# A transformer block on one core: norms written over the projection's output, four row tiles in flight on VectorE, and the last two quarters of the output projection fused

## The chip, the cores and the metric

The kernel runs on one core of one Trainium2 chip. The metric is the device time of one execution in microseconds (us), as the median of several runs. The core's engines are TensorE (PE, matmuls), VectorE (DVE), ScalarE (ACT) and GpSimd (POOL); SyncE (SP) issues the DMAs. SBUF is the memory on the chip, PSUM the small memory that matmuls write.

## What is computed

One layer of a hybrid encoder block in float32: 1024 rows (SEQ) of 1024 channels (D_MODEL), feed-forward width 2816. Three sub-layers follow one another, each between an RMS norm before and an RMS norm behind it, and each is added to the residual stream:

```python
def rms_norm(x, g):
    xf = x.astype(jnp.float32)
    y = xf * lax.rsqrt(jnp.mean(xf * xf, axis=-1, keepdims=True) + EPS)
    return (y * g.astype(jnp.float32)).astype(x.dtype)
...
        f1 = swiglu(rms_norm(h, ffn1_pre_g[l]), ffn1_w_gate[l], ffn1_w_up[l], ffn1_w_down[l])
        h = h + 0.5 * rms_norm(f1, ffn1_post_g[l])
        mix = hybrid_mixer(rms_norm(h, mix_pre_g[l]), positions, w_in[l], b_gate[l],
...
        h = h + rms_norm(mix, mix_post_g[l])
        f2 = swiglu(rms_norm(h, ffn2_pre_g[l]), ffn2_w_gate[l], ffn2_w_up[l], ffn2_w_down[l])
        h = h + 0.5 * rms_norm(f2, ffn2_post_g[l])
```

The mixer projects its input once (`w_in`), runs a latent attention and a dilated windowed attention, merges the two by sigmoid gates and ends with the output projection `merged @ w_out`.

## The kernel before

**Tiling.** The 1024 rows are eight tiles (t = 0 to 7) of 128 rows; a half (hf) is four tiles, 512 rows. All products run in a 32-bit matmul format on numbers split in two, a high and a low part, with three matmuls per product (hi·hi, hi·lo, lo·hi). ScalarE copies the high part, VectorE or GpSimd subtracts it to get the low part. For activations this is `transpose_split` (L418 to L434): TensorE transposes four 128x128 blocks into a PSUM bank, ScalarE writes xh, VectorE writes xl (L433). For weights it is `split`: ScalarE, then GpSimd (L524).

**FFN.** Gate and up products are formed by a scheme of seven products in place of eight over blocks of x (class XS): blocks 0 to 2 are plain pieces of x, blocks 3 to 6 need differences between a tile of the second half and the tile four below it in the first half. For FFN2 the first half's normalised tile is stored in DRAM (xn_d) and read back (xo) for these differences (L416), which go to two slots xt per tile. The down projection accumulates over blocks into the eight output tiles acc (the tile y of the norms). Its last block reads the loads hp; each of its 16 groups of six matmuls is added to acc by VectorE (L1171), and then the tile's norm starts.

**Between two sub-layers** each tile goes through `postnorm` (L474): load the residual (res, SP's queue), ScalarE squares y and sums (L501), GpSimd takes the reciprocal root (L309, L311), the gain is multiplied in (L490) partly by GpSimd and partly by VectorE into a new slot xn, and VectorE forms res = xn · rstd + res (L514, the residual step), which is stored. Then `prenorm` (L436) does the same for the next sub-layer: square (L443), root, and scaling of res with rstd and the next gain. The columns up to `split_at` are scaled by VectorE in pieces (L453), the rest by ScalarE and GpSimd (L459, L460). Last come the transposes and splits of the tile. FFN1's norms (post1) lead to the mixer, the output projection's (`tail`) to FFN2, FFN2's (post2) to the output.

**Output projection** (`outproj`, L2572): for each half four quarters dd of the 1024 input channels. Each quarter gives, per tile and half of the columns, six matmuls into one bank; ScalarE copies the first quarter's result to y, VectorE adds the others (L2560). After the last quarter of a tile, its tail starts. Early products of FFN2 that need only the first tiles (the heads) fill in beside it.

**What sets the order.** The program is written by a planner (class Plan): processes ask for an engine with an estimated duration and a rank, wait for events, and take tokens. A simulated run of them writes the instructions of each engine in one fixed order, and each engine keeps to its order on the chip. `norm_tok` (L1248) holds how many tiles may be in the norms at once: two. `B1` holds four PSUM banks. Pool "u" has 21 slots of 4 KB per partition, for y, x, res, xn, xo, xt, gains and raw weights; an allocation waits until the slot's last user is done, and a load that waits for a slot holds what stands behind it on SP's queue. Constants PRE1 to PRE2 and POOL1 to POOL2 say how many columns of a tile go to which engine:

```python
PRE1, PREM, PRE2 = 768, 768, D
POOL1, POOLM, POOL2 = [512] * 8, [384] * 8, [512] * 4 + [1024, 768, 512, 512]
```

Of the kernel before, what the change touches and what calls it, by code (L numbers as in the profile page):

```python
# [107 lines left out]
PRE1, PREM, PRE2 = 768, 768, D  # L108
POOL1, POOLM, POOL2 = [512] * 8, [384] * 8, [512] * 4 + [1024, 768, 512, 512]
# [4 lines left out]
EARLY = 4  # L114
W0 = 4
# [106 lines left out]
def _build(tc, es, a, consts, out, dbg):  # L222
# [133 lines left out]
    class XS:  # L356
# [25 lines left out]
        def put(self, t, xn, scaled, rank):  # L382
# [7 lines left out]
            if hf == 0:  # L390
                self.nat[j] = (xs, scaled)
                for kb in range(2):
                    spawn(after(scaled[kb], self.block(kb, j, xs[kb])), rank)
                for ev in scaled:
                    yield ev
                if self.late is not None:
                    yield dma(512, lambda: load(xn_d[j * P : (j + 1) * P, :], xn))
            else:
                spawn(after(scaled[1], self.block(2, j, xs[1])), rank)
                old, olds = self.nat[j]  # L400
                if self.late is not None:
                    ob = []

                    def back():
                        o = slot([P, D], name="xo")
                        load(o, xn_d[j * P : (j + 1) * P, :])
                        ob.append(o)

                    yield dma(512, back)
                    old = [ob[0][:, 0:512], ob[0][:, 512:1024]]  # L410
                for ev in (*scaled, *olds):
                    yield ev
                tt = [slot([P, 2, 512], name="xt") for _ in range(2)]
                t1, t2, t3, t4 = tt[0][:, 0, :], tt[0][:, 1, :], tt[1][:, 0, :], tt[1][:, 1, :]
                for i, o, a_, b_ in ((4, t1, xs[0], old[0]), (5, t2, xs[1], t1), (6, t3, xs[1], xs[0]), (3, t4, old[1], t2)):
                    yield dve(512, lambda: V.tensor_sub(o, a_, b_))  # L416
                    spawn(self.block(i, j, o), rank)
# [18 lines left out]
    def prenorm(src, g, X, t, rank, split_at, xn=None):  # L436
# [12 lines left out]
        m = split_at  # L449
        scaled = [Event(), Event((m > 512) + (m < D))]  # L450

        def on_dve(c0, c1, ev):
# [5 lines left out]
        def on_pool(c0, c1, ev):  # L458
            yield act(c1 - c0, lambda: A.mul(xn[:, c0:c1], src[:, c0:c1], rs[0]))  # L459
            yield pool(c1 - c0, lambda: G.tensor_mul(xn[:, c0:c1], xn[:, c0:c1], g()[:, c0:c1]))  # L460
            plan.set(ev)

        spawn(on_dve(0, 512, scaled[0]), rank)
        if m > 512:
            spawn(on_dve(512, m, scaled[1]), rank)
        if m < D:
            spawn(on_pool(m, D, scaled[1]), rank)
# [5 lines left out]
    def postnorm(y, g, res_src, dst, t, box, junk, pool_cols, parts=1):  # L473
# [10 lines left out]

        m = pool_cols(t)
        gained = Event((m > 0) + (m < D))

        def gain_of(cols, eng):
            def write():
                eng.tensor_mul(xn[:, cols], y[:, cols], g()[:, cols])  # L490

            n = cols.stop - cols.start
            yield (pool if eng is G else dve)(n, write)
            plan.set(gained)

        xn = slot([P, D], name="xn")
        box.append(xn)
# [6 lines left out]
        if m:  # L504
            spawn(gain_of(slice(0, m), G), 0)
        if m < D:
            spawn(gain_of(slice(m, D), V), 8)
        yield act(D + 100, sq)
        yield from rstd_steps(bx[0], D, rs)
        yield gained  # L510
        n = D // parts
        for q in range(parts):
            cs = slice(n * q, n * q + n)
            yield dve(n, lambda: V.scalar_tensor_tensor(res[:, cs], xn[:, cs], rs[0], res[:, cs], op0=ALU.mult, op1=ALU.add))  # L514
# [709 lines left out]
    def begin():  # L1224
        def one(t):
# [9 lines left out]
            yield from prenorm(bx[0], lambda: gb["g1"], X1, t, 3, PRE1)  # L1235
# [12 lines left out]
    norm_tok = Tokens(2)  # L1248

    def post1(y, t):  # L1250
# [8 lines left out]
        yield from postnorm(y, lambda: gb["p1"], a["x"], h1, t, bx, lambda: gb["j1"], POOL1.__getitem__)  # L1259
        yield from prenorm(bx[0], lambda: gb["gm"], Xm, t, 3, PREM, bx[1])  # L1260
# [1193 lines left out]
    def merge():  # L2454
# [109 lines left out]
        def tail(y, t, ev):  # L2564
            yield ev
            yield norm_tok
            bx = []
            yield from postnorm(y, lambda: gb["pm"], h1, h2, t, bx, lambda: gb["jm"], POOLM.__getitem__)
            yield from prenorm(bx[0], lambda: gb["g2"], X2, t, 3, PRE2, bx[1])
            plan.release(norm_tok)  # L2570

        def outproj():  # L2572
# [5 lines left out]
            for hf, dd in blocks:  # L2578
                for c in (2 * dd, 2 * dd + 1):
                    yield mts[hf, c][1]  # L2580
                    yield wod[hf, c][1]
                if hf == 1 and dd == 1:
                    plan.set(out_started)
                for j in range(4):
# [3 lines left out]
                    if dd == 0:  # L2588
                        acc[t] = slot([P, D], name="y")
                    for n in range(2):  # L2590
# [4 lines left out]
                        def write():  # L2595
                            bs.ps = bank()
                            terms = []
                            for c in (2 * dd, 2 * dd + 1):
# [4 lines left out]
                        yield pe(6 * 512, write)  # L2603
                        spawn(evac(acc[t], dd == 0, ns, bs.ps, ev), 4)
                    if dd == 3:
                        spawn(tail(acc[t], t, ev), 5)
                plan.release(m_tok, 2)
                plan.release(wd_tok, 2)
# [11 lines left out]
    def post2(y, t):  # L2620
# [5 lines left out]
        yield from postnorm(y, lambda: gb["p2"], h2, out, t, [], lambda: gb["j2"], POOL2.__getitem__, 2 if t == NT - 1 else 1)  # L2626
# [40 lines left out]
```

## Time and profile before

| | us |
|---|---|
| median of 3 runs | 2434.36 |
| lowest and highest run | 2431.82, 2435.98 |
| the profiled execution's own time | 2432.88 |
| its span, first to last instruction | 2430.7 |
| TensorE busy | 2294.6 |
| VectorE busy | 1609.8 |
| ScalarE busy | 1044.0 |
| GpSimd busy | 784.1 |

The profile is of one execution. Its time, 2432.88 us, is its span and 2.2 us around it, and lies 1.5 us under the median. The mean granted clock of TensorE is 0.974 of full speed, 2.4 GHz; the lower level, 0.5, is 1.2 GHz. A row of a timeline gives the start, the duration, the engine, the line of the code, the operation, what it writes and reads, and in brackets how long the engine stood idle before it and what ended that. Several instructions of a kind in a row stand in one row.

### The profile page before, as it was taken

How to read it: one execution, taken by the hardware profiler on the slowest of the kernel's cores; microseconds unless marked ns; L12 is line 12 of the kernel's file. 1: busy time of each engine (PE TensorE's matmuls, PEld its weight loads, DVE VectorE, ACT ScalarE, POOL GpSimd, SP SyncE). 2: the span in 40 equal slices, each digit the busy share in tenths (PEclk: the TensorE clock that was granted, in tenths of full speed). 3: DMA queues.
4: the chain of work that ended last, by engine and by line, in shares of the span. 5: the costliest groups of instructions: out<-in, count | busy, mean ns of one | idle time of the engine just before them, and what ended most of it. 6: DMA issues, size and time to landing. Idle time of an engine off the chain costs nothing. (4 is left out here: it accounts for less than half of the span.)

```text
span 2430.7 us, 30689 instructions
## 1 busy us (share of the span) xinstructions
PE 2294.6 (94%) x11096; PEld 1920.7 (79%) x11096; DVE 1609.8 (66%) x2669; ACT 1044.0 (43%) x1952; POOL 784.1 (32%) x592
## 2 busy tenths in 40 slices
PE   6999999999979999999998898988979999999997
PEld 4788888788869987888886777776868888887885
DVE  7877878875672105666666766347787778778658
ACT  6233434431153336666655545454433334344111
POOL 2000000354274555756532322575300000006443
PEclk9999999999989999999999999999979999999998
DMA  6234434587352133122223222675533444357762
GB/s 186 83 130 139 173 127 163 195 321 254 134 173 70 62 98 100 38 72 65 61 82 90 79 73 85 194 258 180 182 108 113 163 140 173 116 197 280 259 238 104
DMA packets 197145, 350.17 MB, mean 144 GB/s; under 512 B 32577, under 2 KB 112961, under 8 KB 196481
## 3 DMA queue, kind: packets, MB, share of 16 engines
q1 hardware_dynamic: 196992, 348.21, 42.6%
q8 instruction: 87, 1.43, 0.2%
q14 instruction: 66, 0.53, 0.1%
HBM read 234.78 MB, written 113.38 MB: 143 GB/s over the span
## 5 line engine op out<-in xcount | busy, mean ns | idle before, releaser
L706 PE MATMUL s<-xh,wt 128*128 128x512 f32 x1408 | 453.8, 393 | 10.2 <-DVE uu L807 9.0
L524 POOL TENSOR_TENSOR wdb<-rawd,wdb 128x1024 fp32r<-128x1024 f32 x34 | 87.3, 2567 | 892.4 <-ACT wdb L523 889.3
L706 PE MATMUL b<-xh,wt 128*128 128x512 f32 x1056 | 345.7, 394 | 0.7 <-ACT xh L432 0.6
L706 PEld LDWEIGHTS s<-xh,wt 128*128 128x128 f32 x1408 | 266.2, 189 | 69.8 <-DVE uu L807 10.7
L706 PE MATMUL s<-xl,wt 128*128 128x512 f32 x704 | 275.7, 392 | 0.0
L706 PEld LDWEIGHTS b<-xh,wt 128*128 128x128 f32 x1056 | 200.9, 190 | 44.0 <-ACT xh L432 1.0
L706 PE MATMUL b<-xl,wt 128*128 128x512 f32 x528 | 207.7, 393 | 0.9 <-DVE xl L433 0.9
L1134 PE MATMUL b<-wdb,ha 128*128 128x512 f32 x864 | 202.5, 389 | 0.0
L1134 PE MATMUL s<-wdb,ha 128*128 128x512 f32 x816 | 190.5, 389 | 0.0
L1134 PEld LDWEIGHTS b<-wdb,ha 128*128 128x128 f32 x864 | 162.4, 188 | 33.8
L1134 PEld LDWEIGHTS s<-wdb,ha 128*128 128x128 f32 x816 | 153.1, 188 | 31.8
L1495 PE MATMUL b<-xh,wh 128*128 128x512 f32 x384 | 162.7, 424 | 1.4 <-DVE o L2016 0.8
L1966 POOL TENSOR_TENSOR p<-p,rd 128x1024 f32<-128x1024 f32 x64 | 122.5, 1923 | 117.7 <-DVE rd L1963 112.5
L706 PEld LDWEIGHTS s<-xl,wt 128*128 128x128 f32 x704 | 133.3, 189 | 27.4
L1495 PE MATMUL b<-xl,wh 128*128 128x512 f32 x384 | 153.2, 399 | 0.0
L675 ACT CAST wt<-s 128x512 fp32r<-128x512 f32 x176 | 104.2, 617 | 113.9 <-DVE s L635 59.0
L1495 PE MATMUL b<-xh,wl 128*128 128x512 f32 x384 | 152.9, 398 | 0.0
L524 POOL TENSOR_TENSOR wdb<-td,wdb 128x1024 fp32r<-128x1024 f32 x40 | 108.1, 2706 | 109.7 <-ACT wdb L523 98.6
L428 PE MATMUL b<-cst,p 128*128 128x128 f32 x768 | 107.2, 280 | 22.2 <-DVE ptd L433 14.9
L524 POOL TENSOR_TENSOR wl<-raw,wh 128x512 fp32r<-128x512 f32 (+3 forms) x88 | 110.0, 1267 | 53.5 <-ACT wh L523 46.5
L428 PEld LDWEIGHTS b<-cst,p 128*128 128x128 f32 x768 | 90.1, 143 | 40.0 <-DVE ptd L433 17.5
L676 DVE TENSOR_TENSOR wt<-s,wt 128x512 fp32r<-128x512 f32 x176 | 117.9, 684 | 5.4 <-ACT wt L675 5.1
(298 smaller groups left out, 4989.8 us busy)
## 6 DMA issues: line engine op xcount, KB each, us to landing
hs_d<-hl SPq DMA_DIRECT2D x112, 512.0 KB
ha<-hs_d SPq DMA_DIRECT2D x56, 1024.0 KB
raw<-in_ffn_w_gate_dram SPq DMA_DIRECT2D x48, 512.0 KB
raw<-in_ffn_w_up_dram SPq DMA_DIRECT2D x48, 512.0 KB
rawd<-in_ffn_w_down_dram SPq DMA_DIRECT2D x44, 512.0 KB
raw<-in_w_in_dram SPq DMA_DIRECT2D x28, 512.0 KB
h<-res SPq DMA_DIRECT2D x16, 512.0 KB
lg_d<-lg SPq DMA_DIRECT2D x32, 256.0 KB
```

The source lines that it names most:

```text
L428: T.transpose(b[:rows, i * P : (i + 1) * P], src(i), ident)
L524: yield pool(n, lambda: G.tensor_sub(lo, src, hi))
L675: yield act(512, lambda: A.copy(w[:, 0], src))
L676: yield dve(512, lambda: V.tensor_sub(w[:, 1], src, w[:, 0]))
L706: T.matmul(out(), l, r, start=(first and k == 0 and n == 0), stop=(k == 3 and n == 2), skip_group_check=True,)
L1134: T.matmul(ps, l, r, start=(fresh and n == 0), stop=(n == 5), skip_group_check=True)
L1495: T.matmul(bs.ps, l, r, start=(part == 0 and n == 0), stop=(part == 7 and n == 2))
L1966: yield pool(S, lambda: G.tensor_tensor(bx.p, bx.p, bx.rd.broadcast_to([P, S]), op=ALU.mult))
```

## The change

- `prenorm`: VectorE scales all columns in two pieces of 512. ScalarE's and GpSimd's part (L459, L460) and the constants are gone.
- `postnorm`: the gain is multiplied by one VectorE operation over 1024 columns into y itself; the slot xn is gone. The operation is asked for after ScalarE's square, which reads y. The next norm's squares and scaled values are written to y too.
- `norm_tok`: four tiles in the norms at once, not two.
- `XS.put`: two of the four differences are written over the tile read back from DRAM (old), so one slot xt per tile serves, not two.
- `outproj`: in the second half the last two quarters are taken together, 12 matmuls per bank and one addition by VectorE, tile by tile.

Line numbers after it are 21 lower than before from `postnorm`'s end on (1 lower around L428).

```diff
@@ -107,4 +107,2 @@
 
-PRE1, PREM, PRE2 = 768, 768, D
-POOL1, POOLM, POOL2 = [512] * 8, [384] * 8, [512] * 4 + [1024, 768, 512, 512]
 GATES_FROM = 4
@@ -114,2 +112,3 @@
 EARLY = 4
+NORM = 4
 W0 = 4
@@ -412,4 +411,4 @@
                     yield ev
-                tt = [slot([P, 2, 512], name="xt") for _ in range(2)]
-                t1, t2, t3, t4 = tt[0][:, 0, :], tt[0][:, 1, :], tt[1][:, 0, :], tt[1][:, 1, :]
+                tt = slot([P, 2, 512], name="xt")
+                t1, t2, t3, t4 = old[0], tt[:, 0, :], tt[:, 1, :], old[1]
                 for i, o, a_, b_ in ((4, t1, xs[0], old[0]), (5, t2, xs[1], t1), (6, t3, xs[1], xs[0]), (3, t4, old[1], t2)):
@@ -435,3 +434,3 @@
 
-    def prenorm(src, g, X, t, rank, split_at, xn=None):
+    def prenorm(src, g, X, t, rank, xn=None):
 
@@ -448,6 +447,5 @@
         xn = bx[0]
-        m = split_at
-        scaled = [Event(), Event((m > 512) + (m < D))]
+        scaled = [Event(), Event()]
 
-        def on_dve(c0, c1, ev):
+        def scale(c0, c1, ev):
             yield dve(c1 - c0, lambda: V.scalar_tensor_tensor(
@@ -457,12 +455,4 @@
 
-        def on_pool(c0, c1, ev):
-            yield act(c1 - c0, lambda: A.mul(xn[:, c0:c1], src[:, c0:c1], rs[0]))
-            yield pool(c1 - c0, lambda: G.tensor_mul(xn[:, c0:c1], xn[:, c0:c1], g()[:, c0:c1]))
-            plan.set(ev)
-
-        spawn(on_dve(0, 512, scaled[0]), rank)
-        if m > 512:
-            spawn(on_dve(512, m, scaled[1]), rank)
-        if m < D:
-            spawn(on_pool(m, D, scaled[1]), rank)
+        for n in range(2):
+            spawn(scale(512 * n, 512 * n + 512, scaled[n]), rank)
         yield from X.put(t, xn, scaled, rank)
@@ -472,3 +462,3 @@
 
-    def postnorm(y, g, res_src, dst, t, box, junk, pool_cols, parts=1):
+    def postnorm(y, g, res_src, dst, t, box, junk, parts=1):
 
@@ -483,16 +473,4 @@
         res = box[0]
-
-        m = pool_cols(t)
-        gained = Event((m > 0) + (m < D))
-
-        def gain_of(cols, eng):
-            def write():
-                eng.tensor_mul(xn[:, cols], y[:, cols], g()[:, cols])
-
-            n = cols.stop - cols.start
-            yield (pool if eng is G else dve)(n, write)
-            plan.set(gained)
-
-        xn = slot([P, D], name="xn")
-        box.append(xn)
+        box.append(y)
+        gained = Event()
 
@@ -503,7 +481,8 @@
 
-        if m:
-            spawn(gain_of(slice(0, m), G), 0)
-        if m < D:
-            spawn(gain_of(slice(m, D), V), 8)
+        def gain_of():
+            yield dve(D, lambda: V.tensor_mul(y, y, g()))
+            plan.set(gained)
+
         yield act(D + 100, sq)
+        spawn(gain_of(), 2)
         yield from rstd_steps(bx[0], D, rs)
@@ -513,3 +492,3 @@
             cs = slice(n * q, n * q + n)
-            yield dve(n, lambda: V.scalar_tensor_tensor(res[:, cs], xn[:, cs], rs[0], res[:, cs], op0=ALU.mult, op1=ALU.add))
+            yield dve(n, lambda: V.scalar_tensor_tensor(res[:, cs], y[:, cs], rs[0], res[:, cs], op0=ALU.mult, op1=ALU.add))
             spawn(store(dst[t * P : (t + 1) * P, cs], res[:, cs], 512 // parts), 6)
@@ -1234,3 +1213,3 @@
             yield gains0
-            yield from prenorm(bx[0], lambda: gb["g1"], X1, t, 3, PRE1)
+            yield from prenorm(bx[0], lambda: gb["g1"], X1, t, 3)
 
@@ -1247,3 +1226,3 @@
     tail1 = Event()
-    norm_tok = Tokens(2)
+    norm_tok = Tokens(NORM)
 
@@ -1258,4 +1237,4 @@
         bx = []
-        yield from postnorm(y, lambda: gb["p1"], a["x"], h1, t, bx, lambda: gb["j1"], POOL1.__getitem__)
-        yield from prenorm(bx[0], lambda: gb["gm"], Xm, t, 3, PREM, bx[1])
+        yield from postnorm(y, lambda: gb["p1"], a["x"], h1, t, bx, lambda: gb["j1"])
+        yield from prenorm(bx[0], lambda: gb["gm"], Xm, t, 3, bx[1])
         plan.release(norm_tok)
@@ -2567,4 +2546,4 @@
             bx = []
-            yield from postnorm(y, lambda: gb["pm"], h1, h2, t, bx, lambda: gb["jm"], POOLM.__getitem__)
-            yield from prenorm(bx[0], lambda: gb["g2"], X2, t, 3, PRE2, bx[1])
+            yield from postnorm(y, lambda: gb["pm"], h1, h2, t, bx, lambda: gb["jm"])
+            yield from prenorm(bx[0], lambda: gb["g2"], X2, t, 3, bx[1])
             plan.release(norm_tok)
@@ -2577,7 +2556,9 @@
             gb["jm"] = half_slot([P, D], mybir.dt.bfloat16, name="junk")
-            for hf, dd in blocks:
-                for c in (2 * dd, 2 * dd + 1):
+            turns_ = [(0, (d,)) for d in range(4)] + [(1, (0,)), (1, (1,)), (1, (2, 3))]
+            for hf, dds in turns_:
+                cc = [2 * d + u for d in dds for u in range(2)]
+                for c in cc:
                     yield mts[hf, c][1]
                     yield wod[hf, c][1]
-                if hf == 1 and dd == 1:
+                if hf == 1 and dds[0] == 1:
                     plan.set(out_started)
@@ -2587,3 +2568,3 @@
                     ev = Event(2)
-                    if dd == 0:
+                    if dds[0] == 0:
                         acc[t] = slot([P, D], name="y")
@@ -2597,3 +2578,3 @@
                             terms = []
-                            for c in (2 * dd, 2 * dd + 1):
+                            for c in cc:
                                 m, w = mts[hf, c][0].t, wod[hf, c][0]
@@ -2602,8 +2583,8 @@
 
-                        yield pe(6 * 512, write)
-                        spawn(evac(acc[t], dd == 0, ns, bs.ps, ev), 4)
-                    if dd == 3:
+                        yield pe(3 * len(cc) * 512, write)
+                        spawn(evac(acc[t], dds[0] == 0, ns, bs.ps, ev), 4)
+                    if dds[-1] == 3:
                         spawn(tail(acc[t], t, ev), 5)
-                plan.release(m_tok, 2)
-                plan.release(wd_tok, 2)
+                plan.release(m_tok, len(cc))
+                plan.release(wd_tok, len(cc))
             plan.set(out_done)
@@ -2625,3 +2606,3 @@
         yield gains2
-        yield from postnorm(y, lambda: gb["p2"], h2, out, t, [], lambda: gb["j2"], POOL2.__getitem__, 2 if t == NT - 1 else 1)
+        yield from postnorm(y, lambda: gb["p2"], h2, out, t, [], lambda: gb["j2"], 2 if t == NT - 1 else 1)
 
```

Where the order of instructions moves, three places. Each row has its place in the engine's list, the line, the operation, and what it writes and reads.

The first is VectorE at the end of FFN1, tiles 2 to 7. acc are the eight output tiles, b the PSUM banks, p the gain behind FFN1 and gm the gain before the mixer. Before:

```order
766 L1171 TENSOR_TENSOR acc_3881<-acc_3881,b_5113 128x512
767 L453 SCALAR_TENSOR_TENSOR xn_5168<-res_5132,rstd_5237,gm_5093 128x256
768 L490 TENSOR_TENSOR xn_5323<-acc_3857,p_738_5058 128x512
769 L1171 TENSOR_TENSOR acc_3890<-acc_3890,b_5124 128x512
770 L490 TENSOR_TENSOR xn_5333<-acc_3870,p_738_5058 128x512
771 L1171 TENSOR_TENSOR acc_3890<-acc_3890,b_5134 128x512
772 L514 SCALAR_TENSOR_TENSOR res_5289<-xn_5323,rstd_5331,res_5289 128x1024
773 L1171 TENSOR_TENSOR acc_3900<-acc_3900,b_5145 128x512
774 L1171 TENSOR_TENSOR acc_3900<-acc_3900,b_5157 128x512
775 L514 SCALAR_TENSOR_TENSOR res_5292<-xn_5333,rstd_5346,res_5292 128x1024
```

After:

```order
757 L483 TENSOR_TENSOR acc_3850<-acc_3850,p_734_5038 128x1024
758 L1150 TENSOR_TENSOR acc_3870<-acc_3870,b_5114 128x512
759 L493 SCALAR_TENSOR_TENSOR res_5122<-acc_3837,rstd_5177,res_5122 128x1024
760 L1150 TENSOR_TENSOR acc_3880<-acc_3880,b_5124 128x512
761 L1150 TENSOR_TENSOR acc_3880<-acc_3880,b_5136 128x512
762 L493 SCALAR_TENSOR_TENSOR res_5134<-acc_3850,rstd_5189,res_5134 128x1024
763 L1150 TENSOR_TENSOR acc_3889<-acc_3889,b_5152 128x512
764 L1150 TENSOR_TENSOR acc_3889<-acc_3889,b_5167 128x512
765 L451 SCALAR_TENSOR_TENSOR acc_3818<-res_5102,rstd_5198,gm_5073 128x512 x2
766 L451 SCALAR_TENSOR_TENSOR acc_3827<-res_5112,rstd_5222,gm_5073 128x512 x2
767 L451 SCALAR_TENSOR_TENSOR acc_3837<-res_5122,rstd_5229,gm_5073 128x512 x2
```

Scaling pieces stood between the accumulations, and gains of two tiles at a time. Now the gains of the first four tiles and their residual steps stand there, and the scaling pieces of all four follow the last accumulation (b_5167).

The second is TensorE between the output projection and FFN2. wo and mt are weights and merged input of the projection, xh, xl and wt those of FFN2's heads, cst the identity of a transpose. Before:

```order
5260 L285 MATMUL b_15252<-wo_15106,mt_15065 128x512 x3
5261 L285 MATMUL b_15267<-wo_15044,mt_15027 128x512 x3
5262 L285 MATMUL b_15267<-wo_15106,mt_15065 128x512 x3
5263 L706 MATMUL b_15284<-xh_14662,wt_14972 128x512
5264 L706 MATMUL b_15284<-xl_14663,wt_14972 128x512
```

Some forty rows on, where the heads end:

```order
5298 L706 MATMUL b_15303<-xl_14673,wt_15197 128x512
5299 L706 MATMUL b_15303<-xh_14672,wt_15197 128x512
5300 L428 MATMUL b_15391<-cst,xn_15279 128x128 x4
5301 L428 MATMUL b_15401<-cst,xt_15385 128x128 x4
5302 L428 MATMUL b_15410<-cst,xt_15389 128x128 x4
```

After:

```order
5263 L685 MATMUL b_15078<-xl_14602,wt_15063 128x512
5264 L685 MATMUL b_15078<-xh_14601,wt_15063 128x512
5265 L284 MATMUL b_15149<-wo_14811,mt_14766 128x512 x3
5266 L284 MATMUL b_15149<-wo_14889,mt_14815 128x512 x3
5267 L284 MATMUL b_15149<-wo_15007,mt_14984 128x512 x3
```

At the end of the fused block:

```order
5295 L284 MATMUL b_15279<-wo_15007,mt_14984 128x512 x3
5296 L284 MATMUL b_15279<-wo_15069,mt_15014 128x512 x3
5297 L427 MATMUL b_15298<-cst,y_14586 128x128 x4
5298 L427 MATMUL b_15316<-cst,xo_15273 128x128 x4
5299 L427 MATMUL b_15328<-cst,xt_15297 128x128 x4
5300 L427 MATMUL b_15347<-cst,y_14651 128x128 x4
```

The heads stood behind the last quarter's groups and between the first transposes. Now they all stand ahead of the fused block, and the transposes follow it directly.

The third is SP's queue near the end of FFN2. ha and hp are loads of hidden activations (hp those of the last block), res the residual tiles. Before:

```order
785 L999 DMA ha_19710<-hs_d 128x2x1024
786 L999 DMA ha_19744<-hs_d 128x2x1024
787 L1052 DMA hp_19780<-hp_d 128x2048
788 L1052 DMA hp_19844<-hp_d 128x2048
789 L479 DMA res_20069<-h_80 128x1024
790 L471 DMA out_dram<-res_20034 128x1024
791 L479 DMA res_20088<-h_80 128x1024
```

After:

```order
787 L469 DMA res_20026<-h_80 128x1024
788 L978 DMA ha_19622<-hs_d 128x2x1024
789 L469 DMA res_20055<-h_80 128x1024
790 L978 DMA ha_19656<-hs_d 128x2x1024
791 L469 DMA res_20074<-h_80 128x1024
792 L1031 DMA hp_19692<-hp_d 128x2048
793 L1031 DMA hp_19756<-hp_d 128x2048
794 L461 DMA out_dram<-res_19946 128x1024
```

Three residual tiles were loaded ahead of hp and the others behind it, each after a store. Now all eight stand ahead of hp.

## Rows read from the trace of the kernel before

**Rows 1.** Page, part 1: busy us (share of the span) x instructions of each engine.

```profile
PE 2294.6 (94%) x11096; PEld 1920.7 (79%) x11096; DVE 1609.8 (66%) x2669; ACT 1044.0 (43%) x1952; POOL 784.1 (32%) x592
```

**Rows 2.** Windows by stage: window length, busy us per engine (x), PEclk, DMA share, GB/s.

```profile
0.00:60.00 60.00, 38.40 (x170) 28.45 (x171) 47.38 (x79) 37.06 (x69) 14.63 (x28) 0.91 0.63 186
660.00:750.00 90.00, 72.97 (x410) 65.17 (x410) 67.68 (x79) 40.34 (x77) 60.73 (x63) 0.92 0.41 137
1670.00:1710.00 40.00, 31.03 (x132) 24.79 (x131) 31.55 (x33) 22.33 (x39) 25.35 (x21) 0.87 0.67 222
1742.00:1798.00 56.00, 42.35 (x187) 33.32 (x186) 48.12 (x70) 23.98 (x43) 16.42 (x20) 0.76 0.41 142
```

**Rows 3.** Waits of TensorE, 660 to 750 us: total us, times, longest.

```profile
PE b L285 <- DVE xl L433: 6.8, 3, 3.2
PE b L285 <- DVE acc L1171: 3.7, 1, 3.7
PE b L428 <- ACT pj L1410: 3.3, 1, 3.3
```

**Rows 4.** Windows at the lower granted clock, columns as in rows 2.

```profile
684.20:687.60 3.40, 3.40 (x10) 2.63 (x9) 3.40 (x7) 2.42 (x5) 3.23 (x4) 0.51 0.49 130
697.90:701.30 3.40, 3.40 (x18) 3.40 (x18) 2.79 (x4) 3.40 (x7) 3.21 (x4) 0.50 0.10 36
711.60:718.40 6.80, 4.76 (x22) 4.76 (x23) 5.80 (x10) 3.04 (x7) 4.17 (x7) 0.50 0.67 235
1684.40:1687.80 3.40, 3.40 (x9) 2.62 (x9) 3.31 (x3) 1.05 (x2) 1.46 (x2) 0.50 0.28 79
1701.40:1708.20 6.80, 5.52 (x19) 4.80 (x20) 6.34 (x11) 3.42 (x6) 1.76 (x2) 0.50 0.80 242
```

**Rows 5.** Timeline of TensorE, 1764 to 1800 us: start us, us, line, operation, tiles, count.

```profile
1764.30 0.39 PE L706 MATMUL b<-xh,wt 128*128 128x512 f32 x1
...
1793.45 0.78 PE L706 MATMUL b<-xh,wt 128*128 128x512 f32 x1
```

**Rows 6.** L453, scaling pieces: count: ns min/median/max, first and last start, forms.

```profile
L453 DVE SCALAR_TENSOR_TENSOR xn<-x,rstd,g x16: 470/608/1220, 7.4 to 30.6; 128x512 f32<-128x512 f32 x8, 128x256 f32<-128x256 f32 x8
L453 DVE SCALAR_TENSOR_TENSOR xn<-res,rstd,gm x16: 473/852/2822, 680.4 to 735.6; 128x512 f32<-128x512 f32 x8, 128x256 f32<-128x256 f32 x8
L453 DVE SCALAR_TENSOR_TENSOR xn<-res,rstd,g x16: 740/752/2870, 1668.0 to 1783.4; 128x512 f32<-128x512 f32 x16
```

**Rows 7.** L514, residual steps, columns as in rows 6.

```profile
L514 DVE SCALAR_TENSOR_TENSOR res<-xn,rstd,res x25: 747/1285/2878, 670.8 to 2426.5; 128x1024 f32<-128x1024 f32 x23, 128x512 f32<-128x512 f32 x2
```

**Rows 8.** L490, gains on GpSimd and VectorE, columns as in rows 6.

```profile
L490 POOL TENSOR_TENSOR xn<-acc,p x16: 1267/1450/2788, 667.4 to 2419.8; 128x512 f32<-128x512 f32 x14, 128x1024 f32<-128x1024 f32 x1, 128x768 f32<-128x768 f32 x1
...
L490 DVE TENSOR_TENSOR xn<-acc,p x15: 677/680/1110, 668.8 to 2424.5; 128x512 f32<-128x512 f32 x14, 128x256 f32<-128x256 f32 x1
...
L490 DVE TENSOR_TENSOR xn<-y,pm x8: 809/822/1847, 1658.2 to 1776.4; 128x640 f32<-128x640 f32 x8
```

**Rows 9.** Timeline of VectorE, 1755 to 1770 us.

```profile
1765.93 1.88 DVE L433 TENSOR_TENSOR xl<-b,xh 128x512 fp32r<-128x512 f32 x3
```

**Rows 10.** Timeline of TensorE, 2389 to 2416 us: the last FFN2 block.

```profile
2391.51 16.89 PE L285 MATMUL b<-wdb,hp 128*128 128x512 f32 x72
```

**Rows 11.** Waits of TensorE, 1670 to 1710 us.

```profile
PE b L428 <- DVE ga L2521: 5.1, 2, 3.7
```

**Rows 12.** Timeline of VectorE, 2411 to 2431 us.

```profile
2414.03 2.88 DVE L514 SCALAR_TENSOR_TENSOR res<-xn,rstd,res 128x1024 f32<-128x1024 f32 x1
...
2425.86 1.42 DVE L514 SCALAR_TENSOR_TENSOR res<-xn,rstd,res 128x512 f32<-128x512 f32 x2 [0.72 <-POOL rstd L311]
```

**Rows 13.** Timeline of SP's queue, 2345 to 2372 us.

```profile
2359.06 5.81 SPq L1052 DMA_DIRECT2D hp<-hp_d  x2
```

**Rows 14.** Timeline of GpSimd, 2340 to 2400 us.

```profile
2365.68 2.40 POOL L524 TENSOR_TENSOR wdb<-rawd,wdb 128x1024 fp32r<-128x1024 f32 x1 [3.05 <-ACT wdb L523]
```

**Rows 15.** Timeline of GpSimd, 1755 to 1780 us, with the idle time before.

```profile
1771.54 1.00 POOL L490 TENSOR_TENSOR xn<-y,pm 128x384 f32<-128x384 f32 x1 [9.21 <-PE b L428]
```

## The prediction

> **What bounds the kernel now.** I read the page's first part, then the stages of the trace where the change acts, then what TensorE waits for there, then the durations of the operations that change hands. Over the whole span TensorE is busy 2294.6 us of 2430.7 and VectorE 1609.8 [rows 1]: TensorE is the bound, and only its idle time and its slow clock can be won. The change acts in five places, all where eight row tiles are normalised while TensorE has little else:
>
> - A, the start, 0 to 60 us: TensorE 38.4 busy, VectorE 47.4 [rows 2].
> - B, FFN1 to mixer, 660 to 750: TensorE is idle for 90 − 73.0 = 17.0 us. The waits are for the splits of transposes (6.8 us), for a PSUM bank that an accumulation had not yet read (3.7) and for work behind the projection (3.3) [rows 3]. Behind these holes the granted clock is 0.5 (1.2 of 2.4 GHz) for 3.40, 3.40 and 4.76 busy us [rows 4]; half of that, 5.8 us, is lost. In all 22.8.
> - C, the part of the output projection with tiles 0 to 3's norms, 1670 to 1710: idle 40 − 31.0 = 9.0 us [rows 2], and 3.40 + 5.52 busy us at half clock [rows 4], 4.5 lost: 13.5.
> - D, output projection to FFN2, 1742 to 1798: VectorE busy 48.1 of 56, so this one is VectorE's [rows 2]. The last early FFN2 matmul starts at 1764.30, the first product that needs all eight tiles at 1793.45 [rows 5]: 28.8 us after all earlier work is done (1764.30 + 0.39).
> - E, the end, behind the last FFN2 block, bound by VectorE's chain.
>
> **What the operations cost.** VectorE's scaling piece of 512 columns takes 0.74 us alone and up to 2.87, one of 256 columns 0.47 [rows 6]. A residual step of 1024 takes 1.28, up to 2.88 [rows 7]. GpSimd's gain of 512 takes 1.27 to 2.79 (the last is a whole tile), VectorE's 0.68 for 512 and 0.82 for 640 [rows 8]: 0.14 per 128 columns more, so an estimated 0.82 + 3 × 0.14 = 1.25 for 1024, bounded by two of 512 (1.36). Small VectorE operations follow each other every 0.60 us (three in 1.88) [rows 9], TensorE's matmuls every 0.23 (72 in 16.89) [rows 10].
>
> The long values tell why moving work *to* the busier engine can pay: GpSimd's two-input operations and VectorE's hold each other up (2.88 beside 1.28 for the same step). The gains, the main GpSimd work of E, go. **The Trainium skill**, page "SBUF — State Buffer", section "SBUF: two separate sides", has a rule that speaks against the change: a VectorE operation with two SBUF inputs and a GpSimd operation that reads SBUF take one port pair for a whole instruction, and the loser blocks. By that rule each gain moved to VectorE can meet GpSimd's weight splits, which stay; the spread in rows 6 to 8 agrees that they block. By the rule the sum is rival 1's, by the medians the one below.
>
> **Part by part.**
>
> A. VectorE takes 256 columns more per tile: (0.74 − 0.47) × 8 = +2.2. GpSimd's multiply beside it is gone; the slowest piece there is 1.22 [rows 6], so up to 0.48 × 8 = 3.8 is won. Bounds −3.8 + 2.2 = −1.6 and +2.2. I take **−1.5**, the good end, because little else runs on GpSimd there (14.6 of 60 us) [rows 2].
>
> B. The order shows FFN1's last block with fewer VectorE steps between its accumulations, so the 3.7 us bank wait should go; then the transposes of tiles 0 to 3 together, then four products (24 matmuls each), then tiles 4 to 7. Behind the last accumulation VectorE has 8 scaling pieces (5.9), 8 splits (4.8), then for tiles 4 to 7 four gains, four residual steps and 8 pieces (5.0 + 5.1 + 5.9 = 16.0), and some 2 us of reciprocal root: 29 us. TensorE covers it with transposes (some 4) and 96 matmuls of 256 columns, 18 in 3.40 at half clock [rows 4], so 9 to 18: 13 to 22. One idle stretch of 7 to 16, say 12, with 3 of slow clock behind it and 4 of the later waits kept [rows 3] is 19 instead of 22.8: **−4**, bounds −9 and +3. What is late next is tile 7's norm.
>
> C. With four tiles in flight and no second slot per tile, tiles 0 to 3's norms run together beside the next projection group. Of the 13.5 I keep the 5.1 of waits that the trace puts behind gate work, which stays [rows 11], and take the rest as won: **−8.5**, bounds −13.5 and 0.
>
> D. Eight VectorE adds fewer (two quarters in one bank). All early FFN2 heads now run before the fused block of 96 matmuls, 22 us, so nothing is left to cover the norms. VectorE, from 2.8 us into the block (12 matmuls): 8 accumulations 4.8, 4 gains 5.0, 4 residual steps 5.1, 8 pieces 5.3, 13 differences 7.8, 16 splits 9.6 = 37.6, plus some 7.5 of waits for roots: the product starts at 48, 26 us after all earlier work, against 28.8: **−2.5**. Bounds: no waits −10, twice the waits +5. The fused block needs all four quarters' merged tiles and weights first; the 60 head matmuls (13.9 us) ahead hide it. Without them that load is on the path.
>
> E. The last block starts at 2391.51 [rows 10] and its 96 matmuls end 22.7 later, at 2414.2; the last accumulation ends at 2414.9. Then VectorE has two gains, five residual steps and the last tile's two halves: 2.5 + 6.1 + 1.4 = 10.0, to 2424.9. Before it ended at 2425.86 + 1.42 = 2427.3, after a residual step of 2.88 [rows 12]: **−2.5**, bounds −5.5 (three steps, 1.6 each, and a little) and 0.
>
> The gain is written over its own input, so it now waits for ScalarE's square of the same tile. Other tiles' accumulations stand between on VectorE, and the residual step behind it needs the root of that square anyway: at most one gain, 1.25 us, is bare at the last tile of a stage, inside the bounds. GpSimd's roots no longer queue behind gains; I count nothing for that. Differences written over the old copy and one slot less per tile have no price of their own. DMAs: the residual loads move ahead on SP's queue, in E past both loads of the last block (issued from 2359.06, used 32 us later) [rows 10, 13]. They wait for slots of the pool. The weight splits free the last at 2365.68 + 2.40 = 2368.1 [rows 14], 23 us ahead: nothing, by that; else rival 3.
>
> **Sum:** −1.5 − 4 − 8.5 − 2.5 − 2.5 = −19.0 against the profiled run's 2432.88, so 2413.9. That run was 1.5 below the median of three (2434.36), so I forecast **2415.4**. Half-widths of the five terms (2, 6, 7, 7, 3), taken as independent, make 12: 2403 to 2427.
>
> **Rivals.**
>
> 1. *VectorE is held by GpSimd's splits.* GpSimd is busy 60.7 of 90 us in B [rows 2], two thirds of it not gains. If half of B's 32 gains, steps and pieces wait 1.0 (1.85 against 0.82 for the 640 gain) [rows 8], 16 us more on VectorE, half of it for tiles 4 to 7 and bare: B +4. In C half of that, −4.5. Sum −7, **2427**. For: the maxima of rows 6 to 8. Against: most of them lie beside GpSimd's own gains.
> 2. *Four tiles are allowed but not in flight*, because the pool's slots hold them at two. In D GpSimd now stands 9.2 us before a gain at 1771.54, with its input long there [rows 15], which is such a slot. C gains nothing: −10.5, **2424**. Against: each tile needs one slot less.
> 3. *Slower: residual loads block SP's queue.* They stand ahead of the hidden-activation loads of both FFNs' last blocks. It decides if a slot comes over some 20 us late, past the 32 us lead less landing. If it comes only when the block before ends (2391.5), the load lands some 12 us later: 12 + 2 of slow clock in each FFN, +28 on −19: +9, **2443**. Against: the splits' slots come free at 2368.
> 4. *All the idle goes:* A −1.5, B −14, C −13.5, D −5, E −4: −38, **2396**. VectorE's 29 us in B speak against it.
>
> **How the numbers follow.** Forecast 0.48, rivals 0.22, 0.12, 0.13, 0.05. A measurement tells 0.2% (4.9 us) from no change. Faster (below 2429.5): 0.48 + half of rival 1 + most of rival 2 + rival 4 = 0.75; same 0.12 (the other half of rival 1, edges of 2 and 3); slower 0.13. The range 2403 to 2437 leaves out rival 4, a tail below the forecast and most of rival 3.
>
> **What would show it.** In B: no wait for an accumulation's bank, one long wait for tile 4's scaling. In C: no hole over 2 us behind 1670. In D: TensorE idle before the first product with VectorE busy, the product some 11 us earlier. In E: residual steps all near 1.28. VectorE's 1024 gain near 1.25; if over 1.8 in B, rival 1. A wait of a last FFN block's matmul for its load is rival 3. The prediction is wrong if B's idle grows past 23, or D's gap past 34.

## The result, and the profile after

The changed kernel takes 2422.22 us (median of 4 runs, 2421.11 to 2423.15) against 2435.17 for the kernel before: a ratio of 0.9949, 95% interval 0.9932 to 0.9966. That is 13 us less, inside the range and faster as forecast, but 6 us short of the 19 that were summed.

The page's first part of the changed kernel, to set beside [rows 1]:

```profile
PE 2293.0 (95%) x11096; PEld 1921.0 (79%) x11096; DVE 1601.5 (66%) x2662; ACT 1037.9 (43%) x1936; POOL 737.6 (30%) x552
```

TensorE is busy as long as before. VectorE has 8.3 us less, although it took work over, and GpSimd 46.5 us less. The same four windows as [rows 2], the last three moved by 3 to 4 us to hold the same work:

```profile
0.00:60.00 60.00, 38.11 (x175) 29.34 (x176) 47.51 (x81) 34.13 (x62) 8.96 (x20) 0.86 0.61 187
657.00:747.00 90.00, 75.22 (x450) 68.03 (x449) 63.78 (x77) 39.54 (x77) 47.54 (x51) 0.91 0.40 138
1667.00:1707.00 40.00, 33.63 (x152) 26.40 (x150) 34.50 (x38) 22.01 (x39) 23.04 (x16) 0.96 0.75 255
1738.00:1794.00 56.00, 42.78 (x199) 33.64 (x198) 46.30 (x67) 20.73 (x37) 9.94 (x16) 0.88 0.44 152
```

TensorE's idle time fell from 17.0 to 14.8 us at FFN1's junction (B), from 9.0 to 6.4 in the window beside the norms of tiles 0 to 3 (C), and hardly at all in D, where the clock rose instead (0.76 to 0.88). C's window ends inside another hole, though. Over the whole stretch that the table below calls C, TensorE is idle for 9.0 us before and 8.8 after (windows of the kernel before, then of the changed one):

```profile
1664.50:1764.69 100.19, 91.22 (x399) 74.34 (x398) 74.95 (x95) 50.44 (x86) 49.21 (x46) 0.95 0.58 192
1661.20:1760.50 99.30, 90.46 (x395) 72.96 (x394) 71.48 (x85) 45.38 (x78) 40.61 (x34) 0.97 0.51 172
```

TensorE's waits at the junction, in place of [rows 3]:

```profile
PE b L427 <- DVE xl L432: 7.6, 3, 5.0
PE b L427 <- DVE acc L451: 7.2, 4, 2.3
```

The bank wait of 3.7 us, for an accumulation, is gone, as forecast. All waits are now of transposes: for scaled columns (acc is written by L451) and for a split that frees a bank. The low clock, in place of [rows 4], for the same two places (the last stretch lies just behind C's window):

```profile
690.90:694.30 3.40, 2.92 (x14) 2.92 (x15) 3.15 (x6) 2.79 (x5) 2.73 (x3) 0.50 1.06 380
711.30:725.00 13.70, 7.15 (x33) 6.76 (x34) 12.01 (x14) 9.01 (x17) 10.30 (x9) 0.50 0.47 141
1673.90:1677.30 3.40, 3.40 (x10) 2.63 (x9) 3.40 (x3) 0.92 (x2) 3.15 (x3) 0.50 1.05 416
1708.00:1711.40 3.40, 3.11 (x7) 2.48 (x8) 1.94 (x4) 0.77 (x1) 2.37 (x1) 0.50 0.44 145
```

Half of 2.92 + 7.15 is 5.0 us lost at the junction (5.8 before), half of 3.40 + 3.11 is 3.3 in C (4.5 before). Where a stage gained is read from matmuls: both traces have 11096, and outside the moved stretches they stand in the same order, so the start of the same one can be compared. The table below does that, for this kernel and the experiments; a negative number is time won in that stage against the profiled execution of the kernel before.

| kernel | A, to 80 us | FFN1 | B, 660 to 845 | mixer | C | D | FFN2 and end | sum |
|---|---|---|---|---|---|---|---|---|
| **forecast** | −1.5 | 0 | −4 | 0 | −8.5 | −2.5 | −2.5 | −19.0 |
| **the change** | −1.2 | −1.7 | −2.1 | +1.7 | −0.9 | −2.1 | −4.9 | −11.2 |
| e1_vector_gains | +0.8 | −1.7 | −8.6 | −0.2 | −6.0 | +3.2 | −6.2 | −18.6 |
| e2_not_fused | −1.1 | −1.6 | −2.8 | +1.0 | −3.2 | −2.6 | −3.7 | −14.0 |
| e3_two_in_flight | −2.2 | −1.8 | −12.9 | +0.9 | −8.2 | +0.3 | −4.1 | −28.0 |
| e6_two_not_fused | −1.8 | −0.8 | −13.6 | −2.9 | −7.0 | +4.1 | −5.5 | −27.3 |
| e7_three_in_flight | −2.2 | −0.3 | −8.5 | +4.6 | −3.2 | +1.7 | −5.0 | −12.9 |
| e8_four_last_half | −2.5 | −0.3 | −11.8 | −1.5 | −6.9 | −5.0 | −4.3 | −32.2 |
| e9_store_off_sp | −2.3 | −0.4 | −1.7 | −1.3 | −2.1 | −1.4 | −4.0 | −13.2 |
| e11_e8_not_fused | −1.3 | −1.8 | −13.6 | −0.3 | −9.9 | −1.2 | −4.6 | −32.6 |

C goes from the 24 matmuls of a branch projection that start at 1664.50 us before to the end of the last projection or head matmul (1764.30 + 0.39 before [rows 5], 1760.50 after); D from there to the first product that needs all tiles. Each sum is the change of the span. Each row is one profiled execution, and the mixer's column, which no edit touches, runs from −2.9 to +4.6: a difference of some 4 us between two rows in one stage need not be the edit's.

D, timeline of TensorE after the change; the last group of the fused block ends at 1757.83 + 2.66:

```profile
1757.83 2.66 PE L284 MATMUL b<-wo,mt 128*128 128x512 f32 x11
1760.33 0.60 PE L427 MATMUL b<-cst,y 128*128 128x128 f32 x4
1764.07 0.66 PE L427 MATMUL b<-cst,xo 128*128 128x128 f32 x4 [3.13 <-DVE xo L415]
...
1787.14 0.48 PE L685 MATMUL b<-xh,wt 128*128 128x512 f32 x1
```

From 1760.5 to 1787.1 are 26.6 us, where 26 were forecast and 28.8 stood before. The durations of the operations that changed hands, in place of [rows 6 to 8] (ns min/median/max):

```profile
L451 DVE SCALAR_TENSOR_TENSOR xn<-x,rstd,g x16: 741/744/753, 7.2 to 26.2; 128x512 f32<-128x512 f32 x16
L451 DVE SCALAR_TENSOR_TENSOR acc<-res,rstd,gm x16: 739/746/2829, 684.7 to 718.4; 128x512 f32<-128x512 f32 x16
L451 DVE SCALAR_TENSOR_TENSOR y<-res,rstd,g x16: 739/744/1796, 1664.6 to 1775.7; 128x512 f32<-128x512 f32 x16
```

```profile
L483 DVE TENSOR_TENSOR acc<-acc,p x16: 1208/1220/3422, 667.1 to 2410.8; 128x1024 f32<-128x1024 f32 x16
L483 DVE TENSOR_TENSOR y<-y,pm x8: 1216/1220/1226, 1656.0 to 1764.1; 128x1024 f32<-128x1024 f32 x8
```

```profile
L493 DVE SCALAR_TENSOR_TENSOR res<-acc,rstd,res x17: 743/1276/1286, 669.0 to 2415.0; 128x1024 f32<-128x1024 f32 x15, 128x512 f32<-128x512 f32 x2
```

The gain of 1024 columns takes 1.22 us (1.25 was forecast), and the residual step, which had a maximum of 2.88, now has one of 1.29. That is the mutual blocking of VectorE and GpSimd, gone from this operation in this kernel. It is not gone altogether: two scaling pieces at the junction still take 2.49 and 2.83 and one gain 3.42, each beside a weight split of GpSimd. The end, timeline of VectorE:

```profile
2408.40 2.47 DVE L493 SCALAR_TENSOR_TENSOR res<-acc,rstd,res 128x1024 f32<-128x1024 f32 x2
2410.79 1.22 DVE L483 TENSOR_TENSOR acc<-acc,p 128x1024 f32<-128x1024 f32 x1
2411.93 3.80 DVE L493 SCALAR_TENSOR_TENSOR res<-acc,rstd,res 128x1024 f32<-128x1024 f32 x4
```

Two residual steps in 2.47, and the last operation ends at 2415.73, 32.2 us behind the start of the last block at 2383.51, where 33.4 were forecast and 35.8 stood before [rows 10, 12].

### The profile page after: what moved, and what is told of

It reads as the page before. It is cut to its first block, busy times and chain, and to the rows that moved or that the text cites. A ratio compares the mean times of both kernels' runs of the same rounds, so it can differ in the third digit from the quotient of the medians.

```text
span 2419.4 us, 30598 instructions
## 1 busy us (share of the span) xinstructions
PE 2293.0 (95%) x11096; PEld 1921.0 (79%) x11096; DVE 1601.5 (66%) x2662; ACT 1037.9 (43%) x1936; POOL 737.6 (30%) x552
```

## The experiments

Three theories stood at the start, for why C gave so little. S: in the output projection TensorE is held by the supply of weights and gates, so faster norms win little there. N: four tiles in flight is what pays, everywhere. F: the fused block itself took back the gain in C, since the heads move ahead of it. The first three kernels were made to tell them apart, and no theory fits all three. A fourth, the fusion alone on the kernel before (e4_fused_only), could not be built, so what the fusion does there is not known.

**e1_vector_gains**: the kernel before, and only two lines of constants.

```diff
-PRE1, PREM, PRE2 = 768, 768, D
-POOL1, POOLM, POOL2 = [512] * 8, [384] * 8, [512] * 4 + [1024, 768, 512, 512]
+PRE1, PREM, PRE2 = D, D, D
+POOL1, POOLM, POOL2 = [0] * 8, [0] * 8, [0] * 8
```

> The kernel before, with all gains and all scaling on VectorE (the constants set to 0 and 1024), two tiles in flight, separate slots, no fusion. Theory S (in the output projection TensorE is held by the supply of weights and gates, so what the change won is the missing GpSimd work at the start, in FFN1's junction and at the end): -1 at the start, 0 to -2 at the junction, -3 at the end, 2429 to 2431. Theory N (four tiles in flight is what pays, at every junction): only the end gains, 2431 to 2434.

Measured: 2412.94 us, ratio 0.991 (0.989 to 0.993). Both theories miss by far. The two lines alone are worth 22 us, more than the whole change: −8.6 at the junction and −6.0 in C. GpSimd's part was not help with a price but a hindrance. (At the start, A, the same move won nothing here: +0.8.) The scaling pieces and the residual step of the kernel before have medians and maxima of 852 and 2822, 1285 and 2878 ns [rows 6, 7]; here the pieces before the mixer have

```profile
L453 DVE SCALAR_TENSOR_TENSOR xn<-res,rstd,gm x16: 740/744/2339, 677.4 to 729.8; 128x512 f32<-128x512 f32 x16
```

Counted in the timelines: of the 96 scaling, gain and residual operations of VectorE in the kernel before, 33 ran over 0.15 us longer than the shortest of their size, 20 of them beside gains or scaling of GpSimd and 13 beside its weight splits, 34 us in all. In e1 it is 9, all beside splits, 11 us; in the changed kernel 5, 8 us. Besides, VectorE waited 5.1 us at the junction for gains of GpSimd before, and in e1 for none. How the 22 us divide between the blocking and such waits was not taken apart.

**e2_not_fused**: the changed kernel with the last two quarters apart.

```diff
-            turns_ = [(0, (d,)) for d in range(4)] + [(1, (0,)), (1, (1,)), (1, (2, 3))]
+            turns_ = [(0, (d,)) for d in range(4)] + [(1, (d,)) for d in range(4)]
```

> The changed kernel with the last two quarters of the second half taken apart again. Theory S: the first product of FFN2 that needs all tiles comes some 2 us later against the end of the earlier work, 2424 to 2426. Theory F (the fused block itself took back the gain in the output projection, because it pushes the FFN2 heads ahead, where they wait for banks and weights): the hole of 2.6 us at 1706 goes, 2417 to 2420.

Measured: 2418.74 us, ratio 0.9938 (0.9917 to 0.9959). The interval overlaps that of the change. C is 2.3 us shorter and D 0.5. The time lies in theory F's range, but the hole that F names is still there in the trace (2.66 us), so its place is not confirmed; S misses in time and place. Inconclusive by itself.

**e3_two_in_flight**: the changed kernel with two tiles in flight.

```diff
-NORM = 4
+NORM = 2
```

> The changed kernel with two tiles in flight in place of four. Theory S: nothing in the output projection, 1 to 3 us lost at FFN1's junction, 2423 to 2426. Theory N: 6 to 9 us lost over the two junctions, 2428 to 2431.

Measured: 2405.38 us, ratio 0.9882 (0.9862 to 0.9902): 17 us *faster* than the change, where both theories said slower. One number of the change costs 10.8 us at the junction and 7.3 in C. The junction's window in this kernel:

```profile
656.00:746.00 90.00, 83.08 (x504) 76.31 (x503) 67.60 (x83) 41.26 (x82) 43.06 (x53) 0.96 0.41 132
```

TensorE is idle for 6.9 us, not 14.8. The timelines show why. First the changed kernel, whose last FFN1 matmul ends at 684.10:

```profile
685.55 2.64 PE L427 MATMUL b<-cst,acc 128*128 128x128 f32 x16 [1.45 <-DVE acc L451]
689.46 0.66 PE L427 MATMUL b<-cst,acc 128*128 128x128 f32 x4 [1.27 <-DVE xl L432]
691.38 2.82 PE L427 MATMUL b<-cst,acc 128*128 128x128 f32 x12 [1.27 <-DVE xl L432]
```

```profile
719.79 3.67 PE L427 MATMUL b<-cst,acc 128*128 128x128 f32 x16 [5.03 <-DVE xl L432]
```

The transposes of one tile are eight. Those of the first four tiles come together, after the block; then, when the 96 matmuls of four products with them are done (at 705.8), those of four more tiles, with nothing in between. The first of these stand at

```profile
707.22 0.64 PE L427 MATMUL b<-cst,acc 128*128 128x128 f32 x4 [1.42 <-DVE acc L451]
709.90 0.63 PE L427 MATMUL b<-cst,acc 128*128 128x128 f32 x4 [2.04 <-DVE acc L451]
712.82 1.94 PE L427 MATMUL b<-cst,acc 128*128 128x128 f32 x8 [2.30 <-DVE acc L451]
```

and the last sixteen at 719.79. Now two in flight:

```profile
682.82 1.03 PE L427 MATMUL b<-cst,acc 128*128 128x128 f32 x8
...
694.32 0.38 PE L284 MATMUL b<-wh,xl 128*128 128x256 f32 x1 [2.75 <-DVE xl L432]
...
699.98 1.04 PE L427 MATMUL b<-cst,acc 128*128 128x128 f32 x8
...
705.57 1.03 PE L427 MATMUL b<-cst,acc 128*128 128x128 f32 x8
```

The first tile's transposes start straight behind the block, at 682.82, and each later tile's come with products (L284) between. The theory that follows, P: each token more puts more tiles' steps side by side on VectorE, so all of them end late and at once, and TensorE, which could work between them, has nothing.

**e6_two_not_fused, e7_three_in_flight, e8_four_last_half** test P. The first joins the edits of e2 and e3. The second has NORM = 3. The third keeps two tokens and adds two when tile 4's norm starts:

```diff
-NORM = 4
+NORM = 2
...
                     if dds[-1] == 3:
+                        if t == 4:
+                            plan.release(norm_tok, 2)
```

> The changed kernel with two tiles in flight and the last two quarters taken apart. Theory P (four in flight is the cost, and fusion costs some 3 us by pushing the FFN2 heads ahead, however many tiles are in flight): 2401 to 2403. Theory Q (fusion costs only beside four in flight, because there the accumulations stand behind the norms of four tiles; with two it wins eight VectorE additions): 2406 to 2409.

> The changed kernel with three tiles in flight. Theory P (the more tiles are normalised side by side, the later the first one comes and the more transposes come at once): between two and four, 2409 to 2417. Rival T (a threshold: only the fourth tile meets a full pool of slots): as with two, 2404 to 2407.

> The changed kernel with two tiles in flight up to tile 3 of the output projection and four from tile 4 on. Theory P (four in flight costs where other matmuls could lie between the tiles, and wins where nothing else is left): the cost at FFN1's junction and beside the first half goes (11 and 7 us), the 2.4 us won behind the fused block stay: 2401 to 2404. Rival R (four costs everywhere, the shorter tail in the changed kernel came from heads that ended late): 2406 to 2410.

Measured: e6 2405.87 us, 0.9889 (0.9872 to 0.9907); e7 2415.63, 0.9931 (0.9916 to 0.9946); e8 2400.66, 0.9861 (0.9846 to 0.9876). At the junction two, three and four tokens win 12 to 14, 8.5 and 2.1 us: graded, as P says, and no threshold at the fourth. e6 lies between the ranges of P and Q, and its median can't be told from e3's: by the time of the whole kernel the fusion is worth nothing beside two tokens. The table by stage shows more. In C and D together e6 wins 2.9 us and e3, with the fusion, 7.9, which is where Q puts it; e6 gets it back in the mixer and FFN2, which the fusion does not touch. From e1 to e6, which adds the writing over y, the place of the gain behind the square and the single slot xt, the ratio goes from 0.991 to 0.9889; the intervals overlap. e8 is within 0.4 us of P's range and is the fastest kernel of this study, 32 us under the kernel before (2432.86 in the same job). In D four tokens do pay. P's reason, that behind the block there is no work to put between the tiles, is argued and not shown apart. e8's timeline: the last head, and the first product:

```profile
1741.41 0.39 PE L685 MATMUL b<-xh,wt 128*128 128x512 f32 x1
```

```profile
1765.59 0.78 PE L685 MATMUL b<-xh,wt 128*128 128x512 f32 x1
```

That is 23.8 us from the end of one to the start of the other; 29.1 in e3. Without the fusion four tokens win as much there: 27.6 in e11, 32.8 in e6.

**e9_store_off_sp** tests the last rival for C in the changed kernel, where SP's waits in 1640 to 1720 us begin with this one:

```profile
SPq L396 <- DVE y L451: 16.4, 4, 6.5
```

```diff
-                    yield dma(512, lambda: load(xn_d[j * P : (j + 1) * P, :], xn))
+                    yield act(64, lambda: A.dma_start(xn_d[j * P : (j + 1) * P, :], xn))
```

> The changed kernel (four in flight), with the four stores of the first half's normalised tiles issued by ScalarE in place of SP, where they waited 16.4 us for VectorE's scaling ahead of weight loads. Theory P (TensorE has nothing to put between four tiles that come together): the output projection's part with tiles 0 to 3 stays as it is, 2420 to 2424. Rival Q2 (SP's queue, blocked by those stores, held weights and gates back): 5 to 7 us of that part are won, 2415 to 2417.

Measured: 2420.65 us, ratio 0.994 (0.9926 to 0.9955): no change that can be told from the changed kernel. C is 1.2 us shorter, not 5 to 7, so Q2 falls for these stores. SP still waits, now longest behind the residual steps (13.3 us in three waits); what a queue without any such wait would give was not tried.

**e10_one_in_flight**: e8 with NORM = 1, and three tokens released at tile 4. **e11_e8_not_fused**: e8 with the edit of e2.

> The kernel of e8 with one tile in flight in place of two up to tile 3 of the output projection (four behind). Theory P taken to its end (the fewer side by side, the better): 2397 to 2400. Theory P with a limit (the norm of one tile alone takes longer than the 5.5 us in which TensorE makes a tile, so the tiles pile up): 2404 to 2412.

> The kernel of e8 with the last two quarters taken apart. If the fusion is worth something where four tiles' norms end the projection: 2403 to 2405; if not, 2399 to 2402.

Measured: e10 2429.21 us, 0.998 (0.9965 to 0.9994); e11 2401.79, 0.9864 (0.9849 to 0.9879). One tile in flight is some 28 us worse than two, and outside both ranges. TensorE's longest kind of wait at the junction there is

```profile
PE b L427 <- DVE acc L451: 9.5, 3, 3.8
```

for scaled columns again. Tiles now come one at a time and too late: transposes that start at 735.44, 749.02 and 762.95 us, some 14 us apart, each after a wait of 2.1 to 3.5 us. So P has a limit, and two is the best of the four counts here. e11's median can't be told from e8's: what the fusion wins in D there (3.8 us), it loses in C (3.0).

## Why the prediction was right in sign and short in size

**What bounds the kernel**: right. TensorE's busy time moved by 1.6 us; apart from the strays named below, the gains are in the five places and in how late VectorE hands over. That the time lies inside the range is owed to the range's width: the terms sum to −19.0 and the stages to −11.2, and C alone is 7.6 of the difference.

**A** (−1.5): −1.2 measured. The pieces take 744 ns as forecast. That the scaling is what won is not shown: e1 scales the same way there and measures +0.8, and kernels with the changed start lie between −1.1 and −2.5.

**B** (−4): −2.1 measured. Its working holds in the sum: 14.8 us idle and 5.0 of clock, 19.8, where 19 was forecast. Of the idle time 10.8 lie behind the first four products, where one stretch of 12 was forecast; they are four waits of 1.4 to 5.0, the longest for a split and not for tile 4's scaling. The bank wait went. But the step asked only what four in flight cost against the kernel before, and never what two would give with the same edits: −12.9. The 29 us of VectorE work that the sum lists are no fixed price: how much of them is bare depends on the order, 14.8 us of idle time with four tokens and 6.9 with two.

**C** (−8.5): −0.9 measured, inside the term's own bounds but next to nothing. This is the step that failed: "With four tiles in flight and no second slot per tile, tiles 0 to 3's norms run together beside the next projection group." They do run together, and that is the cost: two tokens for these tiles win 6.0 to 7.3 us more in C (e8, e3). The step kept 5.1 us of waits for gate work, took the rest as won and put new waits at nothing. Before, TensorE's other wait here was

```profile
PE b L285 <- DVE xl L433: 3.9, 1, 3.9
```

After, gate work ends only 0.5 us of waits, but these stand in place of the 9.0:

```profile
PE b L427 <- ACT y L2537: 3.0, 2, 2.7
PE b L685 <- DVE y L2539: 2.6, 1, 2.6
PE b L284 <- DVE xl L432: 1.3, 1, 1.3
```

TensorE waits for banks that copies and accumulations (y) have not emptied yet. The longest wait, 2.69 us up to 1671.32, can be followed on ScalarE's timeline:

```profile
1667.32 1.06 ACT L442 ACTIVATE y<-res 128x1024 f32<-128x1024 f32 x1 [2.09 <-DVE res L493]
...
1669.65 1.06 ACT L442 ACTIVATE y<-res 128x1024 f32<-128x1024 f32 x1 [1.18 <-POOL var L308]
...
1670.71 0.56 ACT L2537 COPY y<-b 128x512 f32<-128x512 f32 x1
```

The copy that empties the bank stands in ScalarE's order behind the squares of two tiles' norms, and ScalarE is idle before both squares, waiting for steps of the same norms on other engines. So the norms side by side hold the projection. The 2.64 us hole at 1708.29 is of another kind: the accumulation that ends it stands on VectorE behind gate work (L2502, L2504), so a part of the 5.1 that were kept came back here. It breaks the sign that the prediction set for C, no hole over 2 us behind 1670.

What C wins is not yet won for the kernel, because D, behind it, is bound by VectorE. C and D together give −3.0 in the change, −2.9 in e6, −7.9 in e3 and −11.9 in e8.

**D** (−2.5): −2.1. Right in size by its own count of VectorE's operations, 26.6 us against 26; the product comes 6.3 us earlier, not 11. But "eight VectorE adds fewer" is not what shortened it here: e2, with these additions back, has 26.1. Beside the other token counts the fusion does shorten D, by 3.8 us from e6 to e3 and from e11 to e8. From e3 to the change, two tokens to four, D loses 2.4.

**E** (−2.5): from the start of the last block to the end −3.2. Right, a little small: the two bank waits of 0.42 and 0.77 us in the last block went too. e1, with two tokens and no fusion, wins 3.7 there, so it is the move of the gains that pays.

**What was left at nothing.** Outside the five places −1.7, +1.7 and −1.7 turned up in code that the change does not touch; the last section shows where the first two come from.

**The rivals.** The time is nearest rival 2's 2424, but not by its cause: four tiles were in flight. Rival 1, splits holding VectorE's gains, happened to one gain of 24 (3.42 us, median 1.22) and two scaling pieces, not to half of B's 32 operations. That the two engines can hold each other up so is the rule of the Trainium skill on the shared port (page "SBUF — State Buffer", section "SBUF: two separate sides"). The traces agree, and they speak more *for* the change than against it: GpSimd's gains and scaling were the more frequent partner, 20 of 33 long operations, though at the junction and in C weight splits were, 13 of 21; and e1 shows 22 us from taking that work away. Rival 3 did not come: the last block's loads are issued 32 us before their use, as before [rows 10, 13]:

```profile
2351.06 5.76 SPq L1031 DMA_DIRECT2D hp<-hp_d  x2
```

## What to carry to other kernels

More tiles in flight is no gain by itself: where another engine can work between tiles, finish them early and few at a time (here two; one was too few, by some 28 us); where nothing is left to put between them, more side by side can win, as 5.3 us in D from e3 to e8. Price every number of a change apart, against the best use of the *other* edits and not only against the kernel before: here one edit of two lines was worth 22 us, and one number took 17 back. Moving elementwise work from an idle engine to the busier one can pay when the two hold each other up.

## What was not expected of the hardware

A hole of the same length in code that no edit touches can cost 0 or 2.6 us, by the clock. Inside the mixer TensorE waits for the same split in both kernels, 2.14 us before and 2.07 after (timelines of TensorE, before, then after):

```profile
1535.09 0.76 PE L2304 MATMUL s<-ptd,vv 128*128 128x256 f32 x3 [2.14 <-DVE ptd L433]
```

```profile
1531.21 1.20 PE L2283 MATMUL s<-ptd,vv 128*128 128x256 f32 x3 [2.07 <-DVE ptd L432]
```

The stretch behind it, as windows of the kernel before and of the changed one (the last three columns are the granted clock, the DMA share and GB/s):

```profile
1535.80:1539.20 3.40, 3.40 (x16) 2.80 (x16) 1.22 (x1) 2.54 (x3) 0.62 (x1) 1.00 0.22 82
```

```profile
1532.40:1535.80 3.40, 3.40 (x9) 2.72 (x9) 1.22 (x1) 2.54 (x3) 0.17 (x1) 0.50 0.11 40
```

Before, the clock stayed at 2.4 GHz; after, it fell to 1.2 GHz, with 9 matmuls in 3.4 us where 16 ran before. The change loses 2.6 us there; so do e1, e2, e7 and e10 (2.6 each), e3 and e6 1.9, while e8, e9 and e11 lose nothing. The stray gain in FFN1 is also a matter of what happens to coincide. VectorE's timeline of the kernel before, then of the changed one, at the same three operations:

```profile
464.69 2.83 DVE L864 TENSOR_TENSOR hl<-sg,hl 128x512 fp32r<-128x512 f32 x1
467.45 0.68 DVE L807 TENSOR_TENSOR uu<-s,uu 128x512 f32<-128x512 f32 x1
```

```profile
463.21 0.68 DVE L843 TENSOR_TENSOR hl<-sg,hl 128x512 fp32r<-128x512 f32 x1
463.82 0.68 DVE L786 TENSOR_TENSOR uu<-s,uu 128x512 f32<-128x512 f32 x1
```

The split hl takes 2.83 us where a GpSimd split of a weight runs beside it and 0.68 where it slips in between two. TensorE waits for uu behind it, 4.39 us before and 2.38 + 1.11 after. Nothing there was edited. So of two kernels some 3 us apart the median does not tell what an edit did; a table by stage shows at least whether the difference lies in code that the edit touches.
